# The sine product of the last head group on Vector, and a new set of step times for the attention's operations

## The chip, the core and the metric

The kernel runs on one core of a Trainium2 chip. A core has five engines that this text calls by their names in the profile: TensorE (PE) multiplies matrices and writes its results to PSUM, VectorE (DVE), ScalarE (ACT) and GpSimd (POOL) work elementwise, and SyncE (SP) issues transfers between device memory and the on-chip memory SBUF. ACT and POOL issue transfers as well. Each engine takes its own instructions in order, and an instruction that waits for another engine or for a transfer holds up everything behind it on its engine.

The metric is the device time of one execution in microseconds (us), smaller is better.

## The reference, cut to what matters

The reference is one layer of an encoder over 768 tokens (512 of one request and 256 of another), all in fp32. Half of the input projection's columns go through a Fourier mixing, half through a windowed attention with 16 query heads, 4 key heads and a rotary embedding:

```python
def apply_rope(x, cos, sin):
    half = HEAD_DIM // 2
    x1, x2 = x[..., :half], x[..., half:]
    rot = jnp.concatenate([-x2, x1], axis=-1)
    return x * c + rot * s            # c, s: cos and sin, broadcast over the heads
...
    s = jnp.einsum('bnqhgd,bnkhd->bnhgqk', qb, kb) * scale      # blocks of 128 queries, 384 keys
    m = jnp.maximum(jnp.max(s, axis=-1, keepdims=True), sink_l)
    p = jnp.exp(s - m)
    p = p / (jnp.sum(p, axis=-1, keepdims=True) + jnp.exp(sink_l - m))
    o = jnp.einsum('bnhgqk,bnkhd->bnqhgd', p, vb)
...
    mixed = concatenate([rmsnorm(of, ...), rmsnorm(oa, ...)], axis=-1)
    x = x + mixed @ w_out             # then RMSNorm, squared-ReLU MLP, residual, final RMSNorm
```

The sine product of the title is `rot * s` for the queries of the last of the four head groups.

## The kernel before, in words

Every fp32 matrix product is made from three products of split operands: an operand is copied by ACT to a rounded high part, and DVE subtracts that from the operand to get the low part (`split`, lines 65 and 66). So each operand that reaches TensorE costs one ACT and one DVE instruction first.

The program has stages: the input projection with the Fourier mixing beside it (up to about 397 us), the attention with the first half of the output projection beside it (397 to 620 us), the second half of the output projection, and then the MLP (from 761 us), which takes the rest of the span, some 1859 us. The change lies in the second of these stages.

**The attention stage.** The output projection's first half, which multiplies the Fourier group's output, is cut into 24 slots: 4 column blocks of 512 by 6 token blocks of 128. A slot has 8 steps `k`, and a step is three matmuls (line 821) of 128x512 on TensorE, so there are 192 steps. After each step the program runs the events that are due at that step (`run_events`, called from `proj_slot`). The events are the attention's operations. The attention is cut into 24 units, one for each pair of a query block `b` and a head group `g`; unit `u` starts at step `t = 7.37 u + 4`, and each of its operations has an offset from `t` in steps. For one unit these are:

- `load_q(u + 2)`, `rotate_q(u + 2)`, `split_q(u + 2)`: the queries of the unit after next are loaded by SP (lines 501 and 502 for the groups 0 to 2, whose rotated queries were made ahead; lines 505 to 507 for group 3, whose raw queries `rx` and their swapped halves `ry` are loaded), rotated where `g` is 3, and copied to the operand `qs` (lines 519, 521, 522). The tile `rx` has two buffers, and so has `ry`.
- `qk` for each of 4 heads (line 631): scores into a PSUM tile `s`, of which there are 3. `row_max` (lines 646 and 651, DVE) reads the scores, adds the mask and finds the row's maximum; that frees the `s`. `exps` (line 661, ACT) takes the exponentials, `normalize` (lines 673 and 674 on DVE, line 676 on POOL, four instructions) divides by the sum.
- `trans` (line 688): TensorE turns the probabilities of one key block into a PSUM tile `t` (3 of these, shared with the output `o`); ACT copies the high part `th` (line 691), DVE makes the low part `tl` (line 692).
- `pv` (line 707): the product with the values into `o`; ACT copies one half of it to `ob` (line 716), DVE adds the halves to `os` (line 720), and ACT issues the store of `os` (line 724).

Events that are not tied to a unit: `split_of(m)` splits the Fourier output of token block `m` (lines 65 and 66 with the tiles `ofr`, `ofh`, `ofl`), which `load_of(m)` loads (line 181); `out_split(i)` splits a piece of the output weights (`raw` to `wh` and `wl`) and issues the load of a later piece (lines 75 and 155); `load_oa(m)` loads the finished attention output of block `m` (line 749, tile `oar`), splits it (`oah`, `oal`), squares it on ACT (line 756), adds on POOL (line 757) and sums on DVE (line 760, `sr`) for its norm. A slot's end copies `pm` to `xc` (line 853) and stores it (line 854).

Within this stage SP, ACT, DVE and POOL are recorded in exactly the order in which the events run; TensorE's order is written out as well. Two events due at the same step run in the order of their times. A step time therefore does not say when an operation runs, but only which operations it stands behind and ahead of on its engine. Ahead of the stage, where the loads of the first units are made, SP is under a scheduler, which may move a load forward past others.

`rotate` (lines 449 to 457) is the rotation: the sine product `ry * sinr` on POOL (line 455), the cosine product `rx * cosr` on DVE (line 456), and their sum on DVE (line 457). It is called for the keys and the first three groups' queries ahead of the stage, and by `rotate_q` (line 510) for the units 3, 7, 11, 15, 19 and 23 within it, there on tiles of 64x512.

Of the kernel before, what the change touches and what calls it, by code (L numbers as in the profile page):

```python
# [15 lines left out]
ALU = mybir.AluOpType  # L16
# [4 lines left out]
P = 128  # L21
# [11 lines left out]
HD = 64  # L33
# [7 lines left out]
def hybrid_encoder(ctx: ExitStack, tc: tile.TileContext, a: dict):  # L41
    nc = tc.nc
# [147 lines left out]
    with ExitStack() as ph:  # L190
# [255 lines left out]
            kt["kdh"] = kp.tile([P, NKV, T], F32R, tag="kdh", name="kdh")  # L446
            kt["kdl"] = kp.tile([P, NKV, T], F32R, tag="kdl", name="kdl")

        def rotate(x, y, t0):

            shape = x.shape
            cb, sb = (
                kt[c][: shape[0], t0].rearrange("p (o t) -> p o t", o=1).to_broadcast(shape) for c in ("cosr", "sinr")
            )
            nc.gpsimd.tensor_tensor(out=y, in0=y, in1=sb, op=ALU.mult)
            nc.vector.tensor_tensor(out=x, in0=x, in1=cb, op=ALU.mult)
            nc.vector.tensor_tensor(out=x, in0=x, in1=y, op=ALU.add)

        def rows2(src, s):

            t0 = slice(s * HALF, (s + 1) * HALF)
            x, y = (kt["kp"].tile([P, 1, 512], F32, tag=c, name=c, bufs=n)[:, :, :HALF] for c, n in (("rx", 2), ("ry", 2)))
            z = src[:, t0].rearrange("p (o t) -> p o t", o=1)
            nc.sync.dma_start(x, z)
            for r in range(0, P, 64):
                nc.sync.dma_start(y[r : r + 32], z[r + 32 : r + 64])
                nc.sync.dma_start(y[r + 32 : r + 64], z[r : r + 32])
            rotate(x, y, t0)
            return x[:, 0, :], t0
# [22 lines left out]
        state = {}  # L492
# [17 lines left out]
        def rotate_q(u):  # L510
            b, g = units[u]
            if g == NKV - 1:
                rotate(state[u]["x"][:HD], state[u].pop("y")[:HD], slice(b * P, (b + 1) * P))

        def split_q(u):
            x = state[u].pop("x")
# [95 lines left out]
    op = out_ctx.enter_context(tc.tile_pool(name="op", bufs=1, reuse_waits="tile"))  # L612
# [152 lines left out]
        when(max(t_red, t_sq, t_oa0, t_oa1), reduce)  # L765


    pace, t_first, t_qk, d_qk, t_max, t_exp, t_norm = 7.37, 4, -4.6, 1.75, 0.4, 2.65, 3.7
    t_trans, d_trans, t_th, t_tl, t_pv, d_pv, t_ob, t_os, t_put = 8.9, 1.2, 1.15, 1.5, 16.2, 0, 0.5, 0.1, 1.4
    t_w, t_of, t_xc, t_y, t_oa, t_oa0, t_oa1, t_rot, t_split = 42.4, 5.85, 0, 1.2, 67, 3.6, 5.2, 2.5, 6  # L770
    t_sq, t_red, t_w3, d_w, t_of1, t_of2, t_lof = 6.05, 7.95, 1.65, 2.15, 3.75, 6.5, 15.5
    events, clock = [], [0.0, 0]

    def at(t, fn):
# [11 lines left out]
    for u in range(len(units)):  # L786
        t = pace * u + t_first
        for h in range(4):
            dt = t_qk + d_qk * h
            at(t + dt, lambda u=u, h=h: qk(u, (h,)))  # L790
            at(t + dt + t_max, lambda u=u, h=h: row_max(u, (h,)))
            at(t + dt + t_exp, lambda u=u, h=h: exps(u, (h,)))
        at(t + t_norm, lambda u=u: normalize(u))
        if u + 2 < len(units):
            at(t - 3, lambda u=u: load_q(u + 2))
            at(t - 3 + t_rot, lambda u=u: rotate_q(u + 2))
            at(t - 3 + t_split, lambda u=u: split_q(u + 2))
        for kb in range(3):
            at(t + t_trans + d_trans * kb, lambda u=u, kb=kb: trans(u, kb))
            at(t + t_pv + d_pv * kb, lambda u=u, kb=kb: pv(u, kb))  # L800
# [728 lines left out]
```

## Time and profile before

| | |
|---|---|
| time, median of 3 runs | 2623.02 us (2622.14 to 2624.28) |
| profiled execution | 2622.38 us, of which its span 2620.3 us |
| TensorE busy over the span | 2600.0 us (99%) |
| DVE, ACT, POOL busy over the span | 1736.2, 1075.8 and 251.8 us |
| mean granted TensorE clock | 0.998 of full speed |
| attention stage, 397 to 620 us: TensorE busy | 215.98 of 223.00 us |
| the same stage: DVE, ACT, POOL busy | 170.35, 160.83 and 70.01 us |

The span runs from the first to the last instruction. In a timeline a row has the start in us, the duration in us, the engine, the line, the operation, the tile written and the tiles read with their shapes, the count of merged instructions, and in brackets the engine's idle time before it and what ended it. A row with an engine's name and a `q` (SPq, ACTq) is the issuing of a transfer. A row of waits has who waited, for whom, the total in us, the number of times and the longest. A row of windows has the stretch, its length and each engine's busy time in it with the number of instructions, then the granted TensorE clock, the share of the DMA engines and the GB/s.

### The profile page before, as it was taken

What the parts mean: (1) busy time and instruction counts of PE and PEld (TensorE: products, weight loads), DVE (VectorE), ACT (ScalarE), POOL (GpSimd) and SP (SyncE); (2) the same over time, 40 slices, a digit from 0 to 9 for tenths busy, and PEclk for the clock granted to TensorE, in tenths of its full rate; (3) what the DMA queues carried; (4) which work ended last, traced back from release to release, by engine and by line L of the source; (5) the groups of instructions that cost most, each with busy time, mean ns of one, the idle gap of its engine ahead of it and who ended that gap; (6) DMA issues with size and microseconds to landing.
All of it is one profiled execution on the core that took longest, in us unless ns stands there. A gap on an engine that the chain in (4) does not pass through costs nothing.

```text
span 2620.3 us, 35122 instructions
## 1 busy us (share of the span) xinstructions
PE 2600.0 (99%) x13680; PEld 2378.5 (91%) x13680; DVE 1736.2 (66%) x2176; ACT 1075.8 (41%) x1543; POOL 251.8 (10%) x354
## 2 busy tenths in 40 slices
PE   9999999999999999999999999999999999999998
PEld 9999998887889999999999999988888888888886
DVE  6334447776655655555777777757776765777687
ACT  6233327775333333333454445433333333333335
POOL 1011212333210111000000000010000000000001
PEclk9999999999999999999999999999999999999999
DMA  5323466444673554456666666685543672555364
GB/s 179 120 94 111 136 216 181 117 121 145 208 240 137 174 179 162 155 202 232 208 227 213 220 228 225 208 324 181 184 157 110 211 246 78 178 179 162 98 210 147
DMA packets 254982, 465.16 MB, mean 178 GB/s; under 512 B 20080, under 2 KB 151712, under 8 KB 254176
## 3 DMA queue, kind: packets, MB, share of 16 engines
q1 hardware_dynamic: 189536, 304.24, 36.7%
q10 hardware_dynamic: 53376, 110.97, 11.2%
q0 software_dynamic: 11904, 47.72, 5.4%
q8 instruction: 107, 1.75, 0.3%
q14 instruction: 59, 0.48, 0.1%
HBM read 344.10 MB, written 118.75 MB: 177 GB/s over the span
## 4 chain that ended last, share of the span: by engine, by line
PE 75%; DVE 1%; DMA 1%; issue 0%; ACT 0%; POOL 0%; POOLq 0%; ACTq 0%; SPq 0%; DVEq 0%
PE pu L966 35%; PE pd L1351 34%; PE pm L821 5%; PE ptx L130 0%; DMA sr<-sd 0%; DMA sd<-sm 0%; DMA oar<-oad 0%; DVE sr L760 0%; POOL p L676 0%; DVE acc L1434 0%; ACT oar L756 0%; DVE wl L1340 0%; DVE os L720 0%; DVE tl L692 0%; DVE o L987 0%
## 5 line engine op out<-in xcount | busy, mean ns | idle before, releaser
L966 PE MATMUL pu<-xf,wh 128*128 128x384 f32 x3072 | 783.2, 336 | 0.0
L966 PEld LDWEIGHTS pu<-xf,wh 128*128 128x128 f32 x3072 | 554.6, 188 | 1.5 <-ACT o L984 0.8
L1351 PE MATMUL pd<-wh,sl 128*128 128x512 f32 x1332 | 518.3, 389 | 0.4 <-DVE sl L1341 0.4
L1351 PE MATMUL pd<-wh,sh 128*128 128x512 f32 x1332 | 518.2, 389 | 0.0
L1351 PE MATMUL pd<-wl,sh 128*128 128x512 f32 x1332 | 518.2, 389 | 0.0
L966 PE MATMUL pu<-xf,wl 128*128 128x384 f32 x1536 | 516.1, 336 | 0.0
L1330 ACT ACTIVATE wh<-rd 128x1024 fp32r<-128x1024 f32 x200 | 202.3, 1054 | 522.8 <-PE pd L1351 425.8
L1340 DVE TENSOR_TENSOR wl<-rd,wh 128x1024 fp32r<-128x1024 f32 x200 | 236.0, 1221 | 226.8 <-ACT wh L1330 226.1
L946 ACT ACTIVATE wh<-ur 128x1024 fp32r<-128x1024 f32 x160 | 169.9, 1062 | 372.5 <-PE pu L966 210.7
L1351 PEld LDWEIGHTS pd<-wh,sl 128*128 128x128 f32 x1332 | 250.1, 188 | 52.5 <-DVE sl L1341 0.8
L1351 PEld LDWEIGHTS pd<-wh,sh 128*128 128x128 f32 x1332 | 250.1, 188 | 51.9
L1351 PEld LDWEIGHTS pd<-wl,sh 128*128 128x128 f32 x1332 | 250.1, 188 | 51.9
L966 PEld LDWEIGHTS pu<-xf,wl 128*128 128x128 f32 x1536 | 288.8, 188 | 0.0
L952 DVE TENSOR_TENSOR wl<-ur,wh 128x1024 fp32r<-128x1024 f32 x160 | 195.4, 1222 | 76.2 <-ACT wh L946 76.2
L987 DVE TENSOR_TENSOR o<-pu,o 128x768 f32<-128x768 f32 x160 | 152.8, 956 | 122.5 <-PE pu L966 114.9
L588 PE MATMUL pz<-hh,wh 128*128 128x384 f32 x576 | 147.1, 336 | 0.0
L588 PE MATMUL pz<-hl,wh 128*128 128x384 f32 x576 | 146.3, 334 | 0.0
L588 PE MATMUL pz<-hh,wl 128*128 128x384 f32 x576 | 146.3, 334 | 0.0
L1323 DVE TENSOR_TENSOR rd<-rd 128x1024 f32<-128x1024 f32 x112 | 131.7, 1217 | 0.0
L966 PE MATMUL pu<-xs,wh 128*128 128x384 f32 x512 | 130.4, 336 | 0.0
L946 ACT ACTIVATE wh<-sx 128x1024 fp32r<-128x1024 f32 x64 | 67.9, 1062 | 130.4 <-PE pu L966 105.6
L66 DVE TENSOR_TENSOR wl<-raw,wh 128x1024 fp32r<-128x1024 f32 x56 | 68.3, 1225 | 69.4 <-ACT wh L65 69.1
(228 smaller groups left out, 3725.3 us busy)
## 6 DMA issues: line engine op xcount, KB each, us to landing
rd<-in_w_down SPq DMA_DIRECT2D x176, 512.0 KB, 5.1
ur<-in_w_up SPq DMA_DIRECT2D x128, 512.0 KB, 3.9
sr<-sd SPq DMA_DIRECT2D x95, 384.0 KB, 5.3
pd<-o ACTq DMA_DIRECT2D x60, 384.0 KB, 2.3
o<-pd POOLq DMA_DIRECT2D x60, 384.0 KB, 5.8
sd<-sm ACTq DMA_DIRECT2D x60, 384.0 KB, 2.9
raw<-in_w_in SPq DMA_DIRECT2D x40, 512.0 KB, 3.6
raw<-in_w_out SPq DMA_DIRECT2D x32, 512.0 KB, 4.5
```

The source lines that it names most:

```text
L66: nc.vector.tensor_tensor(out=lo, in0=src, in1=f32(hi), op=ALU.subtract)
L588: nc.tensor.matmul(ps[c][s][:, :HALF], w[:, i, cs], h[j][:, i, s * HALF : (s + 1) * HALF], start=first and n == 0, stop=stop and n == 2,)
L821: nc.tensor.matmul(ps, l(k), w[:, k % 2, :], start=(k == 0 and n == 0), stop=(k == 7 and n == 2))
L946: nc.scalar.activation(wh[:], raw[:], AF.Copy)
L952: nc.vector.tensor_tensor(out=wl[:], in0=raw[:], in1=f32(wh[:]), op=ALU.subtract)
L966: nc.tensor.matmul(ps[:, t, :HALF], w[:, i, t * P : (t + 1) * P], xb[:, o, i, :], start=(s == first_of[bank] and i == 0 and n == 0), stop= ...
L987: nc.vector.tensor_tensor(out=o, in0=src, in1=o, op=ALU.add)
L1323: add = lambda x, y, op: nc.vector.tensor_tensor(out=x[:], in0=x[:], in1=y[:], op=op)
L1330: nc.scalar.activation(wh[:], t[:], AF.Copy)
L1340: nc.vector.tensor_tensor(out=wl[:], in0=t[:], in1=f32(wh[:]), op=ALU.subtract)
L1351: nc.tensor.matmul(ps[m][:, ns], l[:, q, ts], w[:, ns], start=(j == 0 and q == 0 and t == 0), stop=(j == HP // 2 - 1 and q == 1 and t == 2),)
```

## The change

`rotate` gets the engine of the sine product as an argument, POOL by default, and `rotate_q` passes DVE. So in the units 3, 7, 11, 15, 19 and 23 all three instructions of the rotation run on DVE, one behind the other, and POOL has the six sine products no more. Sixteen others, ahead of the stage, stay on POOL.

Fourteen of the step times get new values. As events they are: scores 0.1 step later (`t_qk`, which takes row maxima and exponentials along), normalisation 0.05 earlier (`t_norm`), the second and third key block's turn 0.05 and 0.1 later (`d_trans`), high parts 0.05 later (`t_th`), low parts 0.1 earlier (`t_tl`), the sum `os` 0.1 later (`t_os`), the weight splits 0.05 later (`t_w`), the Fourier splits 1.4 steps earlier for the blocks 3 to 5 (`t_of`) and 0.7 later for block 1 (`t_of1`), the Fourier loads 1.5 steps later (`t_lof`), the store of `xc` 0.2 later (`t_y`), the query operand 0.2 earlier (`t_split`), the squares 0.4 later (`t_sq`), the sums `sr` 0.1 earlier (`t_red`).

```diff
-        def rotate(x, y, t0):
+        def rotate(x, y, t0, engine=nc.gpsimd):
...
-            nc.gpsimd.tensor_tensor(out=y, in0=y, in1=sb, op=ALU.mult)
+            engine.tensor_tensor(out=y, in0=y, in1=sb, op=ALU.mult)
             nc.vector.tensor_tensor(out=x, in0=x, in1=cb, op=ALU.mult)
             nc.vector.tensor_tensor(out=x, in0=x, in1=y, op=ALU.add)
...
-                rotate(state[u]["x"][:HD], state[u].pop("y")[:HD], slice(b * P, (b + 1) * P))
+                rotate(state[u]["x"][:HD], state[u].pop("y")[:HD], slice(b * P, (b + 1) * P), nc.vector)
...
-    pace, t_first, t_qk, d_qk, t_max, t_exp, t_norm = 7.37, 4, -4.6, 1.75, 0.4, 2.65, 3.7
-    t_trans, d_trans, t_th, t_tl, t_pv, d_pv, t_ob, t_os, t_put = 8.9, 1.2, 1.15, 1.5, 16.2, 0, 0.5, 0.1, 1.4
-    t_w, t_of, t_xc, t_y, t_oa, t_oa0, t_oa1, t_rot, t_split = 42.4, 5.85, 0, 1.2, 67, 3.6, 5.2, 2.5, 6
-    t_sq, t_red, t_w3, d_w, t_of1, t_of2, t_lof = 6.05, 7.95, 1.65, 2.15, 3.75, 6.5, 15.5
+    pace, t_first, t_qk, d_qk, t_max, t_exp, t_norm = 7.37, 4, -4.5, 1.75, 0.4, 2.65, 3.65
+    t_trans, d_trans, t_th, t_tl, t_pv, d_pv, t_ob, t_os, t_put = 8.9, 1.25, 1.2, 1.4, 16.2, 0, 0.5, 0.2, 1.4
+    t_w, t_of, t_xc, t_y, t_oa, t_oa0, t_oa1, t_rot, t_split = 42.45, 7.25, 0, 1.4, 67, 3.6, 5.2, 2.5, 5.8
+    t_sq, t_red, t_w3, d_w, t_of1, t_of2, t_lof = 6.45, 7.85, 1.65, 2.15, 3.05, 6.5, 14
```

What this does to the order of the instructions, engine by engine:

- TensorE: one head's scores (two matmuls) stand one step later in the units 5, 7, 9, 11, 13, 15, 17, 19, 21 and 23. The third key block's turn keeps its place in the order.
- DVE: six sine products more. The low part of the Fourier blocks 3, 4 and 5 stands ahead of one row maximum instead of behind it. One normalisation (lines 673 and 674) stands ahead of a weight's low part instead of behind it. Beside unit 23's rotation the sum `sr` stands ahead of `os` instead of behind it.
- ACT: the high parts of the Fourier blocks 2 to 5 stand ahead of one exponential each that was ahead of them, one weight's high part ahead of an exponential and another ahead of a `th`, unit 11's query operand ahead of two squares; near the end of the stage two squares stand behind an exponential. Some stores of `xc` stand one place later.
- POOL: the sine products are gone, the rest keeps its order.
- In the stage behind, one pair of squares and one `sr` change places with a neighbour.
- SP: the two loads of unit 2's queries (lines 501 and 502) stand ahead of two loads of output weights and three of Fourier blocks that were ahead of them. Nothing else moves.

## The prediction

> **What bounds the kernel now.** I read the page first, then TensorE's busy time by stretches, then the waits of TensorE between 385 and 625 us, and last the timelines of all engines around each of those waits.
>
> ```profile
> span 2620.3 us, 35122 instructions
> ```
>
> ```profile
> 397.00:620.00 223.00, 215.98 (x1114) 179.52 (x1113) 170.35 (x498) 160.83 (x385) 70.01 (x108) 0.99 0.45 133
> ...
> 590.00:600.00 10.00, 7.63 (x34) 5.82 (x33) 8.45 (x24) 7.14 (x18) 3.62 (x5) 0.83 0.23 72
> ```
>
> ```profile
> PE s L631 <- DVE mx L646: 4.3, 3, 2.4
> PE t L688 <- POOL p L676: 1.3, 2, 1.2
> PE t L688 <- DVE os L720: 0.9, 1, 0.9
> ```
>
> TensorE bounds the kernel. In the attention stage it is idle for 223.00 - 215.98 = 7.0 us, and 4.3 + 1.3 + 0.9 = 6.5 of these are waits that the table names. One stretch has a mean clock of 0.83, which is (1 - 0.83) x 10 = 1.7 us of TensorE's work lost. So the most that the change can gain is 7.0 + 1.7 = 8.7 us, 0.33%. A loss has no such bound. The question is which of those waits the new order removes, and what it makes late instead.
>
> The profiled execution took 2622.38 us, 2.1 more than its span, and lies 0.64 below the median of 2623.02. I sum against the execution and carry the difference to the median.
>
> **Wait one, 1.16 us at 411: the loads of unit 2's queries.**
>
> ```profile
> 387.48 0.38 SPq L75 DMA_DIRECT2D raw<-in_w_out  x1
> ...
> 395.38 3.88 SPq L501 DMA_DIRECT2D rx<-qh  x1
> ...
> 406.07 0.63 ACT L519 ACTIVATE qs<-rx 128x512 fp32r<-128x512 f32 x1 [2.70 <-DMA rx<-ql]
> ...
> 407.90 0.16 DVE L673 TENSOR_TENSOR rs<-rs,es 128x4 f32<-128x4 f32 x1 [2.74 <-ACT es L666]
> ...
> 408.49 2.87 POOL L676 TENSOR_SCALAR p<-p,rs 128x256 f32<-128x256 f32 x4 [9.02 <-ACT p L661]
> ...
> 410.96 0.78 PE L688 MATMUL t<-ident,p 128*128 128x128 f32 x2 [1.16 <-POOL p L676]
> ```
>
> Read backwards: TensorE waits for POOL's scaling, that for DVE's sum, that for ACT, and ACT stood 2.70 us at the copy of unit 2's queries, whose load SP issued only at 395.38. In the new order these two loads stand ahead of the weight load of 387.48, so the data is there before ACT asks at 406.07 - 2.70 = 403.37. ACT, DVE and POOL come up to 2.7 us earlier, more than the 1.16: gain 1.16. What SP now does later is that weight load, by the two issues and the wait for the stores of the queries that they read; I take 1 to 2 us. Its piece is wanted by TensorE only in step 4, past 400 us, so I cost this at nothing; if that cover went, ACT's weight copy would hold the first exponentials. Next to be late are unit 3's loads, which keep their place.
>
> **Wait two, 0.86 us at 447: unit 7's rotation.**
>
> ```profile
> 435.64 1.23 DVE L66 TENSOR_TENSOR ofl<-ofr,ofh 128x1024 fp32r<-128x1024 f32 x1 [1.01 <-ACT ofh L65]
> ...
> 436.90 0.37 SPq L155 DMA_DIRECT2D raw<-in_w_out  x1
> ...
> 442.95 1.28 POOL L455 TENSOR_TENSOR ry<-ry,sinr 64x512 f32<-64x512 f32 x1 [0.63 <-DMA ry<-zq]
> ...
> 444.27 0.68 DVE L457 TENSOR_TENSOR rx<-rx,ry 64x512 f32<-64x512 f32 x1 [1.42 <-POOL ry L455]
> ...
> 447.53 0.66 PE L688 MATMUL t<-ident,p 128*128 128x128 f32 x4 [0.86 <-DVE os L720]
> ```
>
> The sine product on DVE has no row. The nearest is the cosine product of the same shape:
>
> ```profile
> L456 DVE TENSOR_TENSOR rx<-rx,cosr x6: 682/936/3025, 411.1 to 584.8; 64x512 f32<-64x512 f32 x6
> ```
>
> I take 0.68, its shortest, and keep 3.03 as the other end; on POOL it took 1.28. If `ry` landed at 442.95 as before, DVE's three would run 0.68 + 0.68, and the sum would start 0.09 behind them (the distance of the sum from the end of the cosine product in unit 23, below), at 444.40: 0.13 later than 444.27. So the new engine alone wins nothing here. The step times do. SP issues `rx` and `ry` right behind the weight load of 436.90, which waits for the end of the Fourier block's low part (435.64 + 1.23 = 436.87). That low part stood 1.01 for ACT's high part, which now goes ahead of one exponential, and the low part ahead of one row maximum. I take 1.0 for what this brings the loads forward; then the rotation ends about 0.9 earlier, and the wait of 0.86 goes. Bounds: 0.13 lost, 0.86 won.
>
> **Waits three and four, 0.48 and 1.49 us at 524 and 527 (4.3 - 2.4 in the table): unit 15's rotation.**
>
> ```profile
> 521.76 1.29 POOL L455 TENSOR_TENSOR ry<-ry,sinr 64x512 f32<-64x512 f32 x1 [4.22 <-DMA ry<-zq]
> ...
> 523.08 0.68 DVE L457 TENSOR_TENSOR rx<-rx,ry 64x512 f32<-64x512 f32 x1 [1.62 <-POOL ry L455]
> ```
>
> Here too it is the load that is late, and around it nothing changes place. The sum moves to 521.76 + 0.68 + 0.68 + 0.09 = 523.21. I add 0.13 and leave both waits.
>
> **Wait five, 2.37 us at 593, and the end of the stage: unit 23's rotation.**
>
> ```profile
> 584.35 1.71 POOL L455 TENSOR_TENSOR ry<-ry,sinr 64x512 f32<-64x512 f32 x1
> 586.02 1.30 POOL L757 TENSOR_TENSOR oar<-oar 128x512 f32<-128x512 f32 x1
> ...
> 584.84 3.02 DVE L456 TENSOR_TENSOR rx<-rx,cosr 64x512 f32<-64x512 f32 x1
> ...
> 587.95 0.69 DVE L457 TENSOR_TENSOR rx<-rx,ry 64x512 f32<-64x512 f32 x1
> ...
> 589.82 1.02 DVE L760 TENSOR_REDUCE sr<-oar 128x128 f32<-128x512 f32 x1
> ...
> 589.93 0.62 ACTq L724 DMA_DIRECT2D oad<-os  x1
> ...
> 590.59 0.60 ACT L691 ACTIVATE th<-t 128x512 fp32r<-128x512 f32 x1 [0.63 <-PE pm L821]
> ...
> 591.59 0.69 DVE L692 TENSOR_TENSOR tl<-t,th 128x512 fp32r<-128x512 f32 x1
> ```
>
> The cosine product took 3.02 instead of 0.68 us, and ended at 587.86, 0.54 behind the end of POOL's sum of squares (586.02 + 1.30 = 587.32): DVE stood still while POOL ran its two products. The Trainium skill, SBUF — State Buffer, section Who interferes with whom, says that a DVE instruction with two inputs in SBUF and a GpSimd instruction that reads SBUF lock each other out for a whole instruction; the 3.02 agrees.
>
> Without the sine product POOL still has its sum of squares, ready when ACT's squares are, in the middle of DVE's three. I take it that POOL gets in behind the cosine product, at 584.84 + 0.68 + 0.68 = 586.20, and holds the sum until 587.50 + 0.54 = 588.04, against 588.64: 0.6 earlier. But `sr` (1.02) now stands ahead of `os`, so `os` ends 0.4 later, its store is issued 0.4 later, `th`, which began when that issue was over (589.93 + 0.62), ends at 591.6, and `tl` starts where it did. By itself the rotation gains nothing here. The bounds are 0.2 lost (POOL in ahead of the cosine product) and 1.7 won (POOL not in the way: 588.64 against 584.84 + 2.05).
>
> One thing upstream helps:
>
> ```profile
> 564.93 1.31 DVE L66 TENSOR_TENSOR wl<-raw,wh 128x1024 fp32r<-128x1024 f32 x1 [0.89 <-ACT wh L65]
> ...
> 572.62 0.63 ACT L519 ACTIVATE qs<-rx 128x512 fp32r<-128x512 f32 x1 [1.58 <-DMA rx<-ql]
> ...
> 579.64 0.68 DVE L720 TENSOR_TENSOR os<-o,ob 64x512 f32<-64x512 f32 x1 [2.76 <-DMA oad<-os]
> ```
>
> The weight's high part now goes ahead of a `th` (0.60 each), so its low part, on which SP's next loads wait, comes about 0.5 earlier, and so may the query load, the store of `os` and the `os` at 579.64. I take 0.5 (bounds 0 and 0.6): the chain from 580 on comes 0.5 earlier.
>
> Then the end:
>
> ```profile
> 605.45 0.50 ACT L661 ACTIVATE p<-p,nm 128x256 f32<-128x256 f32 x1
> 606.06 0.58 ACT L716 COPY ob<-o 64x512 f32<-64x512 f32 x1
> ...
> 609.42 2.36 POOL p L676 x4
> ```
>
> POOL's last scaling ends at 611.78, and TensorE uses it at 611.8: the chain of DVE, ACT and POOL from 587 on sets the end of the stage, whatever TensorE waited at 593 and whatever its clock was. In that chain two squares on ACT now stand behind an exponential that needs a row maximum ending at about 605.2, so the exponential and both squares end near 606.9 instead of 606.06, and `ob` with all behind it comes 0.8 later. The price of this place is -0.5 + 0.8 = +0.3.
>
> **What costs nothing.** The rotations of units 3, 11 and 19 move DVE by some tenths and TensorE waits near none of them; their cover is that DVE has idle time there. The ten heads' scores that come one step later are read by DVE later still. Stores of `xc` and the query operands have whole steps of slack. POOL loses 6 x 1.28 us of work; it is not the bound.
>
> **The sum.** -1.16 - 0.86 + 0.13 + 0.3 = -1.6. The execution goes from 2622.38 to 2620.8, the median from 2623.02 to 2621.4.
>
> **The clock.** One stretch ran at half clock right behind the longest wait, and none behind the waits of 1.49 or less. The Trainium skill, TensorE: Matmul & The Clock Gate, Part 1, says that the gate watches free-running windows of 3413 ns and halves the clock after an idle one. By it the half clock could stay away where wait five shrinks, and the 1.7 us with it; in this trace the end of the stage is set by the other chain, so I count nothing.
>
> **The rivals.**
>
> *Faster.* DVE gets through unit 23's rotation ahead of POOL, the squares find slack, and the earlier weight splits bring unit 15's loads forward too. For it: the loads follow DVE's splits everywhere. Against: around unit 15 no order changes. Then -1.16 - 0.86 - 1.2 at the end, and up to 2.0 more: between 2619.8 and 2617.8. Chance 0.22.
>
> *Nothing.* The rotation at unit 7 is still held by its load, the loads of unit 2 are late for another reason, such as the wait for the stores that they read. Then 0.13 + 0.13 + 0.3: 2623.6. For it: two thirds of the sum hang on two transfers. Chance 0.16.
>
> *Slower.* The sine product meets POOL's scaling at unit 23. POOL's work just ahead of the old sine product ended at 584.35, and DVE arrives at 584.84; if DVE comes 0.5 earlier, the first of its three meets POOL's scaling and a later one the sum of squares, each for up to the 2.34 that the cosine product lost. It decides when DVE is there before POOL is done. Price 2.34 on the chain that ends the stage, with the 0.8: 2621.4 + 2.8 = 2624.2, and past +0.2% (5.2 us, about what can be told from no change) only if unit 7 falls to the same and a half clock comes on top. The skill's rule speaks for this one. Chance 0.17.
>
> My forecast has 0.45, with its own range 2620 to 2623. Range for all: 2617 to 2626; below it lies part of the first rival, above it the worst of the last. Faster by over 0.2% is below 2617.8, half of the first rival and a little: 0.14. Slower by over 0.2% is above 2628.3: 0.11, from the last and from a wait that I did not see. The rest, 0.75, is within 0.2%.
>
> **What would show it.** Right: no wait of ACT at unit 2's copy near 403 and none of TensorE at 410; no `os` wait of TensorE near 445; the two waits behind unit 15's rotation still 0.5 and 1.5; `ob` near the end behind two squares, TensorE's last turn waiting for POOL. Wrong: TensorE busy for more than 218 or less than 213 us of the stage; a row of line 455 on DVE much over 0.7; a new waiter on TensorE's list.

## The result, and the profile after

The median of 12 runs went from 2622.86 us (2620.74 to 2625.46) to 2617.32 us (2615.03 to 2619.84). The ratio is 0.9978, with a 95% interval of 0.9971 to 0.9986: 5.5 us less, between 3.7 and 7.6. I had forecast 1.6 less. The time lies inside the range for all cases (2617 to 2626), but below the forecast's own range of 2620 to 2623. The profiled execution took 2618.92 us, 1.6 more than its median; its span is 3.2 us shorter than that of before.

The first line of the page of the changed kernel, its busy time in the attention stage and in the stretch that had been at half clock (columns as before), and the waits of TensorE that lie in the stage:

```profile
span 2617.1 us, 35108 instructions
```

```profile
397.00:620.00 223.00, 217.28 (x1128) 181.17 (x1127) 174.78 (x508) 163.13 (x390) 62.62 (x103) 1.00 0.48 137
590.00:600.00 10.00, 9.66 (x50) 7.73 (x49) 8.47 (x27) 8.24 (x23) 5.45 (x9) 1.00 0.30 93
```

```profile
PE s L631 <- DVE mx L646: 3.8, 3, 1.6
...
PE o L707 <- DVE tl L692: 0.9, 1, 0.9
PE pm L821 <- DVE wl L66: 0.5, 1, 0.5
...
PE t L688 <- POOL p L676: 0.2, 1, 0.2
```

The waits for POOL at 411 and for `os` at 447 are gone, the three for a row maximum are still there, two small ones are new, and no stretch of the stage runs at half clock. Around unit 2, the timeline of the changed kernel:

```profile
389.26 0.58 SPq L501 DMA_DIRECT2D rx<-qh  x1
...
402.34 1.23 DVE L66 TENSOR_TENSOR wl<-raw,wh 128x1024 fp32r<-128x1024 f32 x1 [0.88 <-ACT wh L65]
...
403.62 0.50 PE L821 MATMUL pm<-wl,ofh 128*128 128x512 f32 x1 [0.55 <-DVE wl L66]
...
404.70 0.62 ACT L519 ACTIVATE qs<-rx 128x512 fp32r<-128x512 f32 x1
...
410.00 0.68 PE L688 MATMUL t<-ident,p 128*128 128x128 f32 x4
410.43 0.48 PE L821 MATMUL pm<-wh,ofh 128*128 128x512 f32 x1
```

SP issues the load 6.1 us earlier than at 395.38, ACT copies the queries without a wait, and TensorE's four turns run in one go, 0.43 us to the next product. Before, the same four turns took from 409.12 to 411.50:

```profile
409.12 0.69 PE L688 MATMUL t<-ident,p 128*128 128x128 f32 x2
...
411.50 0.48 PE L821 MATMUL pm<-wh,ofh 128*128 128x512 f32 x1
```

That is 2.38 us, 1.95 more, though the row of the wait says 1.16: the modelled length of the first two matmuls covers the rest. Here the idle time in the row is less than what TensorE loses.

Unit 7's rotation, unit 15's and 23's, and the end of the stage, in the timeline of the changed kernel:

```profile
433.47 0.57 SPq L505 DMA_DIRECT2D rx<-zq  x1
...
440.14 0.92 DVE L455 TENSOR_TENSOR ry<-ry,sinr 64x512 f32<-64x512 f32 x1
...
441.70 0.68 DVE L457 TENSOR_TENSOR rx<-rx,ry 64x512 f32<-64x512 f32 x1
...
519.05 0.68 DVE L455 TENSOR_TENSOR ry<-ry,sinr 64x512 f32<-64x512 f32 x1 [3.43 <-DMA ry<-zq]
...
524.21 0.39 PE L631 MATMUL s<-kdl,qs 128*128 128x256 f32 x1 [1.50 <-DVE mx L646]
...
582.75 0.68 DVE L456 TENSOR_TENSOR rx<-rx,cosr 64x512 f32<-64x512 f32 x1
...
582.98 1.60 POOL L757 TENSOR_TENSOR oar<-oar 128x512 f32<-128x512 f32 x1 [1.29 <-ACT oar L756]
...
583.46 1.67 DVE L457 TENSOR_TENSOR rx<-rx,ry 64x512 f32<-64x512 f32 x1
...
585.70 1.08 DVE L760 TENSOR_REDUCE sr<-oar 128x128 f32<-128x512 f32 x1
...
586.70 0.68 DVE L720 TENSOR_TENSOR os<-o,ob 64x512 f32<-64x512 f32 x1
...
589.27 0.39 PE L631 MATMUL s<-kdl,qs 128*128 128x256 f32 x1 [1.60 <-DVE mx L646]
...
601.21 1.14 ACT L756 ACTIVATE oar<-oar 128x512 f32<-128x512 f32 x2
...
602.37 0.59 ACT L716 COPY ob<-o 64x512 f32<-64x512 f32 x1
...
613.13 1.07 DVE L760 TENSOR_REDUCE sr<-oar 128x128 f32<-128x512 f32 x1 [0.26 <-POOL oar L757]
...
614.12 0.68 DVE L692 TENSOR_TENSOR tl<-t,th 128x512 fp32r<-128x512 f32 x1
...
614.86 0.50 PE L707 MATMUL o<-tl,vhl 128*128 128x512 f32 x1 [0.91 <-DVE tl L692]
```

Unit 7's loads leave 3.9 us earlier and its rotation finds its data there. Unit 15's load is as late as before. At unit 23 POOL's sum of squares got in behind the cosine product, and the sum ended 0.55 behind it (584.58 to 585.13), as forecast.

TensorE's order of work is the same but for some scores, so the stage can be cut at its products with the values (line 707), and the stretches compared, in us. The second columns are further profiles of the same two kernels, from the experiments.

| from, to (times of before) | before | before again | changed | changed again |
|---|---|---|---|---|
| start to the first scores, 397.56 | 397.56 | 397.38 | 397.60 | 397.06 |
| to the first product with the values, 418.51 | 20.95 | 22.97 | 19.83 | 18.90 |
| to 442.95 | 24.44 | 24.41 | 24.44 | 24.44 |
| to 452.55 (unit 7's rotation) | 9.60 | 8.70 | 8.53 | 8.53 |
| to 490.25 | 37.70 | 37.65 | 37.36 | 37.34 |
| to 536.51 (unit 15's) | 46.26 | 46.15 | 46.06 | 45.02 |
| to 583.53 | 47.02 | 47.02 | 47.02 | 47.20 |
| to 618.00 (unit 23's, and the end) | 34.47 | 34.12 | 34.02 | 33.42 |
| to the end of the span | 2002.34 | 2002.37 | 2002.28 | 2002.33 |

The difference lies in the stage. In the means of the two profiles of each kernel the span is 4.9 us shorter, and 2.6 of that lie in the first part. There an execution of before differs from the next by 2.0 us, more than the 1.1 between the two kernels in the profiles first compared.

### The profile page after: what moved, and what is told of

Read it like the earlier page. It is cut to its first block, busy times and chain, and to the rows that moved or that the text cites. A ratio compares the mean times of both kernels' runs of the same rounds, so it can differ in the third digit from the quotient of the medians.

```text
span 2617.1 us, 35108 instructions
## 1 busy us (share of the span) xinstructions
PE 2598.2 (99%) x13680; PEld 2376.9 (91%) x13680; DVE 1735.9 (66%) x2182; ACT 1076.0 (41%) x1543; POOL 245.7 (9%) x348
## 4 chain that ended last, share of the span: by engine, by line
PE 75%; DVE 1%; DMA 1%; issue 0%; ACT 0%; POOL 0%; ACTq 0%; POOLq 0%; SPq 0%; DVEq 0%
PE pu L966 35%; PE pd L1351 34%; PE pm L821 5%; PE ptx L130 0%; DMA sr<-sd 0%; DMA sd<-sm 0%; DMA oar<-oad 0%; DVE acc L1434 0%; DVE sr L760 0%; DVE wl L1340 0%; DVE o L987 0%; ACT o L994 0%; ACT o L995 0%; ACT jk L1270 0%; ACT oar L756 0%
```

## The experiments

Times are medians; ratios are to the kernel before, run beside them on the same chip. The experiments ran in three groups, each on its own chip: the first four; then the second profile of before, the changed kernel with unit 2's loads put back, the one with the loads eight steps ahead and the first of the two on the new orders; then the other four. The kernel before had medians of 2622.84, 2621.67 and 2622.66 us beside them, so a difference of two times from different groups can be off by a microsecond; where it matters, the difference of the two gains over the kernel before stands beside it. "First part" is the stretch of the second row above.

**Each half of the change.** Theory A said that the step times carry the gain, by two pairs of loads brought forward; its rival B, that the engine does. The engine alone, on the kernel before:

```diff
-        def rotate(x, y, t0):
+        def rotate(x, y, t0, engine=nc.gpsimd):
...
-            nc.gpsimd.tensor_tensor(out=y, in0=y, in1=sb, op=ALU.mult)
+            engine.tensor_tensor(out=y, in0=y, in1=sb, op=ALU.mult)
...
-                rotate(state[u]["x"][:HD], state[u].pop("y")[:HD], slice(b * P, (b + 1) * P))
+                rotate(state[u]["x"][:HD], state[u].pop("y")[:HD], slice(b * P, (b + 1) * P), nc.vector)
```

> The kernel before with one edit: the sine product of the six rotations in the stage runs on DVE, all step times as before. Theory A (the step times carry the gain; they do it by bringing two pairs of loads forward): TensorE's waits at 411 (1.16 us) and at 447 (0.86 us) stay, those at 524 and 527 stay, and only unit 23's rotation may end 0.6 us earlier, so that the wait at 593 shrinks from 2.37 to 1.8 or so; time between 2621.0 and 2623.0, at most 1.9 us below the kernel before. Rival B (the engine carries it: POOL's products held DVE in every rotation, and the half clock behind the wait at 593 goes with them): 3 us or more below the kernel before, 2619.8 or less, and no stretch of half clock in the stage.

Measured: 2620.89 us, ratio 0.9992 (0.9983 to 1.0001). The wait at 593 shrank to 1.87, the half clock stayed. The profiled execution was the slowest of its kind: its first part took 25.87 us, with two waits of 1.0 and 1.15 near 411 and 6.8 us at half clock from 411.94 on. It also has a wait of 0.71 for a weight's low part at 403.11, though unit 2's loads stand at their old place there. And the step times alone, the changed kernel with

```diff
-                rotate(state[u]["x"][:HD], state[u].pop("y")[:HD], slice(b * P, (b + 1) * P), nc.vector)
+                rotate(state[u]["x"][:HD], state[u].pop("y")[:HD], slice(b * P, (b + 1) * P))
```

> The changed kernel with its sine product put back on POOL: all fourteen step times new, the engine as before. Theory A: no wait at 411, none at 447, 2618 to 2620.5, so at least half of the 5.5 us; of unit 23 the cosine product takes 3 us again, and os, which now stands behind sr, comes later than before, so the wait near 590 is 2.5 us or more and a half clock follows it. Rival B: the step times alone give 2 us or less, 2620.9 or more.

Measured: 2619.69 us, 0.9989 (0.9980 to 0.9998), first part 18.90, no wait at 411 or 447, a wait of 2.12 near 588, where I had expected 2.5 or more, and the half clock behind it. Neither half carries all of it: 2.1 and 2.9 us, which add up to about the whole, each with an interval of some 2.4 us to either side.

**Which step time.** On the kernel before, one value each:

```diff
-    t_sq, t_red, t_w3, d_w, t_of1, t_of2, t_lof = 6.05, 7.95, 1.65, 2.15, 3.75, 6.5, 15.5
+    t_sq, t_red, t_w3, d_w, t_of1, t_of2, t_lof = 6.05, 7.95, 1.65, 2.15, 3.75, 6.5, 14
```

> The kernel before with t_lof = 14 alone: it moves only the two loads of unit 2's queries on SP, ahead of two weight loads and three Fourier loads. Theory A: the wait at 411 goes and one of some 0.5 us for a weight's low part comes near 403.6; as the changed kernel's products stand 1.08 us earlier at 418, this gives 1.1 us, 2621.8. Rival C (a wait costs its idle time only, so 1.16 gained and 0.55 lost): 0.6 us. Rival D (the gain is given back at the next late load, unit 7's, which does not move): TensorE stands 1.1 us earlier at 418 and no earlier at 450 than in the kernel before, time unchanged.

```diff
-    t_w, t_of, t_xc, t_y, t_oa, t_oa0, t_oa1, t_rot, t_split = 42.4, 5.85, 0, 1.2, 67, 3.6, 5.2, 2.5, 6
+    t_w, t_of, t_xc, t_y, t_oa, t_oa0, t_oa1, t_rot, t_split = 42.4, 7.25, 0, 1.2, 67, 3.6, 5.2, 2.5, 6
```

> The kernel before with t_of = 7.25 alone: the splits of the Fourier blocks 3 to 5 come 1.4 steps earlier. Theory A: SP's load of unit 7's queries follows the split of a Fourier block, so the rotation comes about 1 us earlier, the wait at 447 (0.86 us) goes and that at 411 stays; 0.9 to 1.4 us below the kernel before, 2621.5 to 2622. Rival: the wait at 447 goes only because everything ahead of it came earlier through unit 2's loads, and here it stays: time unchanged within 0.3 us.

Measured: `t_lof` alone 2620.19 us, 0.9990 (0.9981 to 0.9999), first part 20.33; `t_of` alone 2622.70, 1.0001 (0.9992 to 1.0009), first part 23.24 with 3.4 us at half clock. So the load of unit 2 seems worth more than the 1.1 us that its wait showed, though the interval reaches down to 0.3; the splits by themselves are worth nothing that can be measured, although their profile has no wait at 447 (the wait went as theory A had it, the time stayed as the rival had it). The two slow first parts, both with unit 2's loads at their old place, raised the question whether the one profile of before that the prediction read was typical.

**The kernel before once more, and the changed kernel with unit 2's loads put back.**

> The kernel before once more, unchanged, for a second profile of it. From the first scores of the stage to the first product with the values, TensorE took 20.95 us in the profile shown of before; with one edit that leaves unit 2's loads where they are it took 25.87 and 23.24, each time with 3.4 or 6.8 us at half clock behind the wait near 411; with those loads moved forward it took 19.83, 18.90 and 20.33, never at half clock. Theory E (the early wait costs the kernel before more in most executions than in the one profiled): here 22 us or more, with a half clock between 410 and 425. Rival F (the edits made those two slow): 20.9 to 21.2, no half clock there.

The waits in the timeline of this second execution of before, and its busy time in four windows (the column behind POOL's count is TensorE's clock):

```profile
406.30 0.63 ACT L519 ACTIVATE qs<-rx 128x512 fp32r<-128x512 f32 x1 [3.11 <-DMA rx<-ql]
...
409.25 0.79 PE L688 MATMUL t<-ident,p 128*128 128x128 f32 x2 [0.16 <-POOL p L676]
...
411.19 0.79 PE L688 MATMUL t<-ident,p 128*128 128x128 f32 x2 [1.15 <-POOL p L676]
```

```profile
409.23:412.64 3.41, 1.97 (x8) 1.27 (x9) 2.53 (x5) 2.00 (x6) 3.41 (x4) 1.00 1.08 304
```

```profile
413.00:414.00 1.00, 1.00 (x5) 0.70 (x4) 0.69 (x2) 0.00 (x0) 0.28 (x1) 0.50 1.17 293
414.00:415.00 1.00, 1.00 (x7) 1.00 (x6) 0.93 (x5) 0.97 (x2) 0.00 (x0) 0.50 0.35 105
415.00:416.00 1.00, 1.00 (x4) 0.81 (x4) 0.97 (x2) 1.00 (x5) 0.00 (x0) 0.50 0.00 0
```

2622.71 us, first part 22.97: theory E. ACT waited 3.11 instead of 2.70 for the same load, and a half clock of 3.4 us followed from 412.64 on, 1.7 us of work, which the first profile did not have. The other test, on the changed kernel:

```diff
-    t_sq, t_red, t_w3, d_w, t_of1, t_of2, t_lof = 6.45, 7.85, 1.65, 2.15, 3.05, 6.5, 14
+    t_sq, t_red, t_w3, d_w, t_of1, t_of2, t_lof = 6.45, 7.85, 1.65, 2.15, 3.05, 6.5, 15.5
```

> The changed kernel with t_lof = 15.5 again: unit 2's two loads go back to their place on SP, all else is new. Theory E (the early loads are worth 1.1 us in the profile, and 2 to 4 in the median because of the half clock behind the wait): 2.0 to 4.0 us slower than the changed kernel, 2619.3 to 2621.3; the wait near 410 is back, with 21 us or more from the first scores to the first product with the values. Rival G (only the idle time counts, 1.16 lost and the wait of 0.55 at 403.6 won): 0.6 us, 2617.9.

Measured: 2621.53 us, 1.0001 (0.9992 to 1.0010), first part 23.53. That is 4.2 us above the changed kernel's median, or 5.4 by the gains over the kernel before (0.1 against 5.5): theory E, past its upper end. Without the early loads nothing of the gain that can be measured is left.

**Unit 15's loads.** The waits that the change leaves at 521 and 524 come from a load behind three loads of weights on SP. In the changed kernel:

```diff
-            at(t - 3, lambda u=u: load_q(u + 2))
+            at(t - (8 if units[u + 2][1] == NKV - 1 else 3), lambda u=u: load_q(u + 2))
```

> The changed kernel with the loads of rx and ry of the last head group (units 3, 7, 11, 15, 19, 23) eight steps ahead of their unit instead of three: on SP they stand ahead of one to three loads of weights or attention output. Theory J (the waits of 0.65 and 1.50 near 521 and 524 are nothing but unit 15's late load: SP stands behind three weight loads): both waits go, TensorE gains 2.2 us or a little more there, 2614.5 to 2615.2. Rival K (the load meets the weight loads in the DMA queues anyway, or a weight piece is late instead): 1 us or less, and a new wait of TensorE for a weight's low part past 520.

The issue in the timeline of this kernel, 5.9 us earlier than at 510.64 in the changed one, and all that the table of TensorE's waits still names in the stage:

```profile
504.73 0.57 SPq L505 DMA_DIRECT2D rx<-zq  x1
```

```profile
PE o L707 <- DVE tl L692: 0.8, 1, 0.8
...
PE t L688 <- POOL p L676: 0.2, 1, 0.2
```

Measured: 2613.26 us, 0.9970 (0.9959 to 0.9982), 4.1 below the changed kernel, or 2.9 by the gains over the kernel before (8.4 against 5.5). The stretch to 536.51 took 43.10 us instead of 46.06, so the two waits of 0.65 and 1.50 had cost 3.0 (and the one of 1.38 in the second profile of the changed kernel 1.9). The wait near 589 is gone as well: the edit brings unit 23's loads forward too, and the stretch from 583.53 on took 31.98 instead of 34.02 and 33.42. Theory J, and more than it asked for, since it named unit 15 alone.

**The same step back on that kernel, two edits on the kernel before, and the changed kernel again.** The first is that kernel with `t_lof = 15.5`:

> The kernel with the loads eight steps ahead, with t_lof = 15.5 again, so that unit 2's two loads go back to their place. Theory E: 3 to 5 us slower than that kernel (2613.3), 2616.3 to 2618.3, with two waits of about 1 us each near 410 and a half clock behind them in the profile. Rival G (the loads are worth what their wait shows, 1.16 us and less): 2614.5 or less.

```profile
409.31 0.78 PE L688 MATMUL t<-ident,p 128*128 128x128 f32 x2 [1.13 <-POOL p L676]
...
411.17 0.33 PE L688 MATMUL t<-ident,p 128*128 128x128 f32 x1 [1.08 <-POOL p L676]
```

Measured: 2617.62 us, 0.9979 (0.9970 to 0.9989), 4.4 us slower, or 3.4 by the gains over the kernel before (5.0 against 8.4); first part 23.67, with these two waits and 3.4 us at half clock behind them. Either way unit 2's loads are worth more than rival G's 1.16. The second is the kernel before with `t_lof = 14` and the engine:

> The kernel before with two edits: t_lof = 14, and the six sine products on DVE; the other thirteen step times old. Theory E (the early loads carry 3.9 us on average, the engine 0.3 near 455 and a little at unit 23, the other step times about 1): 4 to 5 us below the kernel before, 19 to 20.4 us in the first part of the stage, and the wait and the half clock near 593 still there. Rival L (each edit alone gave 2 to 3 us, and they overlap): 3 us or less below the kernel before.

Measured: 2617.80 us, 0.9980 (0.9971 to 0.9989), first part 18.90: these two edits give the whole gain, and the thirteen other step times together none that can be measured. The half clock near 593 did not come (I expected it); one came from 524.76 to 528.18 instead, behind waits of 0.88 and 1.49. What the engine does at unit 23, first in the kernel with the early loads alone and then in this one, is seen in a timeline and a window of each:

```profile
582.86 3.01 DVE L456 TENSOR_TENSOR rx<-rx,cosr 64x512 f32<-64x512 f32 x1
584.04 1.28 POOL L757 TENSOR_TENSOR oar<-oar 128x512 f32<-128x512 f32 x1
...
590.75 0.48 PE L631 MATMUL s<-kdl,qs 128*128 128x256 f32 x1 [2.30 <-DVE mx L646]
```

```profile
590.00:594.00 4.00, 3.25 (x9) 2.67 (x10) 3.86 (x15) 2.76 (x8) 2.35 (x4) 0.61 0.22 65
```

```profile
583.81 0.67 DVE L456 TENSOR_TENSOR rx<-rx,cosr 64x512 f32<-64x512 f32 x1
584.04 1.61 POOL L757 TENSOR_TENSOR oar<-oar 128x512 f32<-128x512 f32 x1 [1.28 <-ACT oar L756]
584.52 1.67 DVE L457 TENSOR_TENSOR rx<-rx,ry 64x512 f32<-64x512 f32 x1
...
590.33 0.39 PE L631 MATMUL s<-kdl,qs 128*128 128x256 f32 x1 [1.04 <-DVE mx L646]
```

```profile
590.00:594.00 4.00, 3.29 (x15) 2.44 (x16) 3.86 (x15) 3.18 (x8) 2.40 (x4) 1.00 0.17 50
```

The wait falls from 2.30 to 1.04 and the half clock goes; from the product at 583.53 to the one at 618.00 it takes 32.90 instead of 34.13 us. This is the old order, with `os` ahead of `sr`. In the new order the pair is the step times alone against the changed kernel: a wait of 2.12 with a half clock against 1.60 and 1.00 without one, and 34.46 us against 34.02 and 33.42. On the kernel before, with unit 2's loads late, the engine left the half clock and won next to nothing here, 34.34 against 34.47 and 34.12. And unit 7, where `t_of` is old in this kernel:

```profile
440.59 0.69 DVE L455 TENSOR_TENSOR ry<-ry,sinr 64x512 f32<-64x512 f32 x1 [1.01 <-DMA ry<-zq]
...
445.18 0.66 PE L688 MATMUL t<-ident,p 128*128 128x128 f32 x4 [0.63 <-DVE os L720]
```

The load is late again and the stretch takes 9.36 us, against 8.53 in the changed kernel (from which this one differs in twelve more step times). The last of the three, unchanged:

> The changed kernel once more, unchanged, for a second profile and for times beside those of the next three. Theory E (forward loads of unit 2 leave no wait near 411 and no half clock there; the wait of 0.55 at 403.6 belongs to single executions): from the first scores of the stage to the first product with the values 18.9 to 20.4 us, no half clock before 580, 5 to 6 us below the kernel before. Rival: 21 us or more with a half clock, so that the early loads only lower the odds.

Measured: 2617.00 us, 0.9979 (0.9970 to 0.9988), first part 18.90, without the wait at 403.6 and without a half clock.

**The new orders at unit 23 and at the end.** First in the changed kernel, then in the one with the loads eight steps ahead:

```diff
-    t_sq, t_red, t_w3, d_w, t_of1, t_of2, t_lof = 6.45, 7.85, 1.65, 2.15, 3.05, 6.5, 14
+    t_sq, t_red, t_w3, d_w, t_of1, t_of2, t_lof = 6.05, 7.95, 1.65, 2.15, 3.05, 6.5, 14
```

> The changed kernel with t_sq = 6.05 and t_red = 7.95 again: near unit 23 os stands ahead of sr once more, and at the end of the stage two squares stand ahead of an exponential. Theory H (sr in front of os delays th, and with it tl, by about 1 us; this is the wait of 1.60 near 590): that wait shrinks to 1 us or less and TensorE comes 0.5 to 1 us earlier at 603; at the end of the stage the wait of 0.91 for the last low part goes or stays with the order of sr. Time 0.5 to 1.5 us below the changed kernel. Rival I (the two orders give and take the same): within 0.3 us of it.

> The kernel with the loads eight steps ahead, with t_sq = 6.05 and t_red = 7.95 again. Theory H (with sr ahead of os the last low part comes 0.8 us late, which is the last wait of the stage): the wait of 0.75 near 608.6 goes, about 1 us below that kernel, 2612.2, and 3.7 or so per thousand below the kernel before. Rival I: the wait is replaced by one for POOL's last scaling, as in the changed kernel with these two values alone (0.55): within 0.4 us of it.

Measured: 2617.24 us, 0.9983 (0.9974 to 0.9992), and 2612.84 us, 0.9960 (0.9948 to 0.9973). In the profiles the wait for the last low part went in both, a wait of 0.55 for POOL's scaling came in its place, and the stretch from 583.53 on took 32.75 us instead of 34.02 and 33.42, and 31.64 instead of 31.98. So the two orders cost TensorE 0.3 to 1.3 us there; in the times that can't be told from nothing, as rival I had it. The last kernel is the fastest of all: 0.9960 against the changed kernel's 0.9979 beside it.

The first part in all profiles:

| unit 2's loads | first part, us | half clock in it |
|---|---|---|
| at their old place | 20.95, 22.97 (before); 25.87, 23.24, 23.53, 23.67 | none; 3.4; 6.8, 3.4, 3.4, 3.4 us |
| moved forward | 19.83, 18.90 (changed); 18.90, 20.33, 18.90, 18.90, 18.90, 18.90 | none in any |

The means are 23.37 and 19.20, 4.2 us apart. The medians of the four pairs that differ by this step alone are 2.7 apart on the kernel before, 3.1 with the engine, 4.2 in the changed kernel and 4.4 in the one with the loads eight steps ahead; by the gains over the kernel before on the same chip they are 2.7, 2.9, 5.4 and 3.4. The mean is 3.6 both ways. The engine, by the same reckoning, is worth 2.0 us on the kernel before, 2.2 with the early loads beside it and 2.4 with all the new step times.

## Why the prediction was right in part, and where it failed

**Wait one** was the right mechanism with the wrong size. The step that failed is "gain 1.16". It is about 4 us (3.6 by the times, 4.2 by the first parts). Two things were missing. The idle time of a row is not the cost: 1.16 stood for 1.95. And the one execution read was the mildest of six: ACT's wait for unit 2's load was 2.70 there and 2.79 to 3.43 in the other five, where TensorE waits twice and a half clock follows. The load left SP at 395.38, behind five others, with nothing to spare; moved forward, ACT finds its data in all eight profiles.

**The delayed weight load**, costed at nothing: no run shows its price by itself. TensorE waited 0.55 for a weight's low part at 403.62 in one of two profiles of the changed kernel, and the first part took 19.83 us there, against 18.90 in the other. But the kernel with the engine alone, where nothing moved on SP, waited 0.71 for the same product. What these two share is that the last weight load ahead of the stage left SP late, at 395.28 and 395.51 (and at 395.59 with `t_lof` alone, where TensorE waited 0.37 and 0.15); it left at 393.77 in before and at 393.11 in the second profile of the changed kernel, which have no such wait. Why one execution issues it 2 us later than the next stays open.

**Wait two.** The mechanism is right, and the gain about the size forecast. In the six profiles with the new `t_of` and the loads three steps ahead, the one with `t_of` alone among them, unit 7's load leaves SP 16.0 us behind the first product with the values; in the five with the old value it is 16.6 to 18.8. In the pair first compared that is 2.8 us (437.36 to 433.47, with TensorE 1.1 earlier) where I took 1.0. Where TensorE is early the stretch took 9.0 and 9.4 with the old value and 8.53 in the changed kernel, up to 9.36 - 8.53 = 0.83; that the other step times have no part in this is not shown. But it was no gain to be added to the first. In the second profile of before, and in the four others with a long first part, the stretch took 8.5 to 8.7 us with either value of `t_of`. Whoever loses 2 us at 411 arrives after the load. The early loads uncover this wait, and the Fourier splits take it away again.

**Waits three and four** stayed, as said, at 0.65 and 1.50 in the profile first read; the second has one of 1.38 alone. That "the load is late" was right; that it could be moved I did not ask. Moving the loads of this head group was worth 3 to 4 us, of which 1.9 to 3.0 lie in unit 15's stretch and the rest at unit 23.

**Wait five and the end.** POOL's entry behind the cosine product came as forecast. From the time DVE reaches the rotation to the end of its sum it took 2.98 us instead of 3.80 (582.15 to 585.13, and 584.84 to 588.64), 0.8 less where I had 0.6. "By itself the rotation gains nothing here" failed: in the changed kernel's own order the engine shortens the wait by 0.5 to 1.1 and the stretch by 0.4 to 1.0, and where `os` stays ahead of `sr` the wait falls by 1.26 and the stretch by 1.2, each time without the half clock. "So I count nothing" for the clock is in doubt at the same place: the five profiles with a half clock there took 34.1 to 34.5 us for the stretch, the nine without it 31.6 to 34.0; how much of that is the clock's no run separates. The end's +0.8 was about right: the last four products took 1.78 and 1.68 us in the changed kernel, 0.74 and 0.81 before, and with the two orders put back the whole stretch is shorter by 0.3 to 1.3. It shows as a wait for a low part behind `sr`, not for POOL. That the weight splits bring 0.5 was not tried by itself.

**The signs.** The signs for wait one, wait two and unit 15 came, and `ob` stands behind two squares. Not as foreseen: TensorE's last wait is for a low part instead of POOL, two new waiters are on its list (the low parts at 403.62 and 614.86), and the sine product took 0.92 at unit 7.

**The sum.** -1.6, with -3.0 more for wait one (4.2 for 1.16), -1.2 more for the engine at unit 23, and 0.7 less for wait two (8.70 to 8.53 instead of 0.86), is -5.1, against -5.5 measured. These terms are from single profiles, and the engine's is from the old order, so the close agreement is in part luck. The bound of 8.7 for any gain failed in the same way, since it was made from one execution and from idle times: the fastest kernel is 9.8 below the kernel before beside it. The case with 0.75, "within 0.2%", is not settled: 0.9978 lies just outside, and its interval reaches to both sides. That the time lies inside the range for all cases, 0.3 us from its end, is luck, since most of what carried it was not in the sum. Of the rivals, *Faster* was nearest, its lower end 0.5 us above the result, but for another reason than it gave: unit 15's loads did not move. *Slower* did not come: DVE's sine product at unit 23 took 0.68.

## What to carry to other kernels

Where TensorE waits for a chain that begins with a transfer issued just in time, read two executions before pricing the wait: the row gives a lower bound, and a slightly later load can add a stretch at half clock that costs more than the wait. Moving a small load ahead of large ones on its queue is the cheap repair, and the next such load, with its wait in plain sight, is the next gain; the engine change beside it was worth about 2 us, and the fine reordering nothing that could be measured.

## What the runs showed of the hardware

Whether a wait halves the clock depended on where it lay. Waits near 590 of 1.87, 2.12, 2.24, 2.30 and 2.37 us were followed by a half clock, those of 1.60 and less were not; near 411 two waits of 0.16 and 1.15 were, and one of 1.16 was not; waits of 0.88 and 1.49 near 524 were in one kernel, and of 0.65 and 1.50 not in another. In the trace's record of the clock a halving lasted 3.413 us, or twice that, and the full clock before the first one lasted 402.773, 406.186, 518.826 or 583.679 us, which is 118, 119, 152 and 171 times 3.4133: the clock is judged on a fixed grid. The Trainium skill, TensorE: Matmul & The Clock Gate, Part 1, states such a free-running window of 3413 ns, and the trace agrees. It also says that the clock is halved after an idle window; here the window need not be idle, since in the 3.41 us ahead of the halving in the second profile of before TensorE was busy for 1.97 (first window row above).

On that grid the limit can be read off. Give each matmul the time at which the next one follows it at full clock when nothing waits (0.23 us for those of lines 821 and 707, 0.12 for line 631, 0.11 for line 688), and add up which share of each window is filled. In the attention stage the 14 profiles have 913 windows at full clock. The 11 that were filled to 0.38 or less were each followed by a half clock, and none of the 902 filled to 0.44 or more was. Of the twelve windows at half clock, the one filled to 0.40 was followed by another, the eleven filled to 0.53 or more by the full clock. So what decides here is what one window loses in all, not the longest wait: the second profile of before filled its window to 0.36, with 8 matmuls, and the first one, whose wait of 1.16 shares its window with less other loss, to 0.54, with 11:

```profile
409.84:413.25 3.41, 2.16 (x11) 1.67 (x12) 2.18 (x6) 1.19 (x3) 3.22 (x3) 1.00 1.15 319
```

A DVE product that waits for POOL ended 0.54 to 0.55 us behind POOL's, in the changed kernel (585.13 against 584.58) as in the pair at unit 23 (586.19 against 585.65), and where POOL was idle when it began, the cosine product took 0.67 instead of 3.01. That is the exclusive port which the Trainium skill, SBUF — State Buffer, section Who interferes with whom, describes; that DVE needs another half microsecond after POOL's end is shown by these rows.
